# Own weight tiles for chunks of seven products, and a third such chunk in each gate unit

## The chip, the cores and the metric

The kernel runs on one core of one Trainium2 chip. The core has TensorE (PE: matmuls and transposes, which write to PSUM), VectorE (DVE), ScalarE (ACT), GpSimd (POOL) and SyncE (SP, which here issues the loads of weights). Each engine takes the instructions of its own queue in the order in which the program wrote them; this kernel writes that order by hand (`manual_schedule`). The metric is the device time of one execution in microseconds. All times are from the profiled execution or from the table of runs.

## The reference, cut to what matters

One layer of an encoder on 256 tokens with 2048 channels, in float32:

```python
x = x + 0.5 * swiglu(rmsnorm(x, n1), w_gate1, w_up1, w_down1)   # FFN 1, 5632 hidden
...                                                             # mixers: pooling and convolution branches
x = x + 0.5 * swiglu(rmsnorm(x, n2), w_gate2, w_up2, w_down2)   # FFN 2, 5632 hidden
return rmsnorm(x, n_final)

def swiglu(h, w_gate, w_up, w_down):
    return (silu(h @ w_gate) * (h @ w_up)) @ w_down
```

The change touches the two FFNs alone.

## The kernel before

**High and low halves.** Every float32 operand of a matmul is split in two: a high half (a cast to the matmul's type, by ScalarE, L153) and a low half (source minus high, by VectorE, L155). A product is three matmuls: high by high, high by low, low by high. The function is `hi_lo`.

**Chunks.** All weights stream through as chunks of two rows of 128 x 1024 (`raw`, five tiles of 512 KB, loaded by SP two chunks ahead). `run` goes over the stream: at step i it issues the load of chunk i+2, splits chunk i+1 (`split_chunk`), runs the functions that `at(i, ...)` has put aside for this step, and then issues the matmuls of chunk i (`run_chunk`). What `amid(i, ...)` has put aside comes in the middle of these, after the 12th matmul of chunk i. The high and low tiles of a chunk's rows (`wh`, `wl`) have four buffers each, which is two chunks: the split of chunk i+1 waits until TensorE has left chunk i-1.

**Eights and sevens.** An ordinary chunk multiplies two 128-row slices of the activations by a 128 x 1024 weight row each, for two halves of the tokens: eight products of 128 x 128 by 128 x 512, 24 matmuls (L256). A chunk listed in `SEVEN` is taken as a product of 2 x 2 blocks by a scheme with seven products, 21 matmuls (L277). Its price is paid by the other engines: `split_seven` forms three sums of weight blocks with four additions on VectorE (L193, tiles `sum`, in place in `raw` too), then splits row 0, the three sums (`exth`, `extl`, 128 x 1536) and row 1, in this order. The activations need four differences as well, the *E forms* (`e_forms`, L307, then split into `xE` or `hE`), once per FFN. Four of the seven products are shared by several results: they are collected in PSUM banks 0 to 3 (`P1`, `P5`, `P6`, `P7`) over all sevens of a unit, and after the last one `shared_parts` combines them (L427 and L432) into two `part` tiles. The other three products go straight to the accumulators in banks 4 to 7. In a seven the shared products come first (12 matmuls, in the order `P1`, `P5`, `P6`, `P7`; the second matmul of `P6` is the first to need `extl`), except in the first unit after an ordinary one (`u.start`), where they come last.

**Units.** An FFN is a stream of units: eleven gate units (u = 0 to 10, eight chunks each, 512 columns of gate and of up), and down units in between. Gate unit 0 has eights alone; units 1 to 10 have sevens at chunks 0 and 2. After units 4 and 8 come two down units each (eight chunks, sevens at 0 and 2), and after unit 10 the last two (six eights each).

**The end of a gate unit** (`gate_done_seven`): VectorE adds the accumulators of each token half to `part` (L413, 128 x 1024), ScalarE applies silu (L414), VectorE multiplies to the hidden values `h` (L418). The next gate unit transposes them back on TensorE (`put`, L343): two groups of four transposes, into banks `P6` and `P1` as soon as `shared_parts` has read them. Each is split into `ht` by ScalarE and VectorE. For two hidden slices of each four units (u % 4 = 0 and 1, first group) a copy `hy` is made from the same bank (L389) and E forms of it follow at once. `gate_early` puts these two groups at the heads of the two chunks after the one at which it runs; it runs at the step after the unit's last seven, so now they stand at the heads of chunks 4 and 5.

Of the kernel before, what the change touches and what calls it, by code (L numbers as in the profile page):

```python
# [8 lines left out]
F32 = mybir.dt.float32  # L9
F32R = mybir.dt.float32r  # L10
# [3 lines left out]
P = 128  # L14
D = 2048
T = 256
# [10 lines left out]
W2 = 2 * C  # L27
KD = D // P
# [11 lines left out]

GROUP = 4
SEVEN = (0, 2)

B_P1, B_P5, B_P6, B_P7, B_11, B_12, B_21, B_22 = range(8)

# [36 lines left out]
def encoder_kernel(ctx: ExitStack, tc: tile.TileContext, x, xT, vecs, rows, pool_m,  # L82
# [7 lines left out]
    stg = ctx.enter_context(tc.tile_pool(name="stg", bufs=2))  # L90
# [13 lines left out]
    ps = psp.tile([P, 8, C], F32, name="ps")  # L104
# [5 lines left out]
    stream = []  # L110
    side, middle = {}, {}

    def at(i, fn):

        side.setdefault(i, []).append(fn)

    def amid(i, fn):

        while isinstance(stream[i][0], Special):
            i += 1  # L120
        middle.setdefault(i, []).append(fn)
# [6 lines left out]
    def add_unit(u):  # L128
        for cc in range(u.k // 2):
            stream.append((u, cc))  # L130
# [21 lines left out]
    def hi_lo(src, h, l=None):  # L152
        nc.scalar.copy(out=h, in_=src)  # L153
        if l is not None:
            nc.vector.tensor_tensor(out=l, in0=src, in1=h.bitcast(F32), op=ALU.subtract)  # L155
        return h, l

    def stream_tiles(i, kk):
        return (wsp.tile([P, W2], F32R, tag="wh", name=f"wh{i}_{kk}"),
                wsp.tile([P, W2], F32R, tag="wl", name=f"wl{i}_{kk}"))  # L160
# [26 lines left out]
    def split_seven(i, r0, r1):  # L187

        w11, w12, w21, w22 = r0[:, :C], r0[:, C:], r1[:, :C], r1[:, C:]
        sm = ffn["pool"].tile([P, 3, C], F32, tag="sum", name=f"sum{i}")  # L190

        def add(out, a, b):
            nc.vector.tensor_tensor(out=out, in0=a, in1=b, op=ALU.add)  # L193
        add(sm[:, 1, :], w12, w22)
        add(w12, w11, w12)
        add(sm[:, 0, :], w12, w22)
        add(sm[:, 2, :], sm[:, 0, :], w21)
        ext = tuple(ffn["pool"].tile([P, 3, C], F32R, tag=f"ext{x}", name=f"ext{x}{i}") for x in "hl")
        return (hi_lo(r0, *stream_tiles(i, 0)), hi_lo(sm, *ext), hi_lo(r1, *stream_tiles(i, 1)))

    def bank(name):
        Pos.bank += 1
# [79 lines left out]
    def pair(pool, tag, n, name):  # L282

        r = []
        for b in range(n // 4):
            h, l = (block(pool, f"{tag}{s}{b}", F32R, f"{name}{s}{b}") for s in "hl")
            r += [(h[:, q, :], l[:, q, :]) for q in range(4)]
        return r

    def block(pool, tag, dtype, name):  # L290
        return pool.tile([P, 4, T], dtype, tag=tag, name=name)

    def hidden(pool, name):

        return [tuple(block(pool, f"h{s}{u}", F32R, f"{name}{s}{u}") for s in "hl") for u in range(GROUP)]

    def e_tiles(pool, tag, n):

        return {c: tuple(pool.tile([P, 4, P], F32R, tag=f"{tag}E{x}{c}", name=f"{tag}E{x}{c}_{n}") for x in "hl")
                for c in SEVEN}  # L300

    def e_forms(dst, even, odd):

        e = stg.tile([P, 4, P], F32, tag="sg", name=f"e{Pos.now}")
        a11, a21, a12, a22 = even[:, :P], even[:, P:], odd[:, :P], odd[:, P:]
        for n, (a, b) in enumerate(((a11, a21), (a21, a22), (a11, e[:, 1, :]), (a12, e[:, 2, :]))):
            nc.vector.tensor_tensor(out=e[:, n, :], in0=a, in1=b, op=ALU.subtract)  # L307
        hi_lo(e, *dst)
# [16 lines left out]
    def lhs_of(pairs):  # L325
        def f(k, t):
            h, l = pairs[k]
            return h[:, t * P:(t + 1) * P], l[:, t * P:(t + 1) * P]
        return f
# [8 lines left out]
    def transposes(src_of, n, name, b=None):  # L338

        b = bank(name) if b is None else b  # L340
        for j in range(n):
            for t in range(NT):
                nc.tensor.transpose(out=b[:, j * T + t * P: j * T + (t + 1) * P],  # L343
                                    in_=src_of(j, t), identity=ident)
        return b
# [22 lines left out]
    ffn = {}  # L368

    def open_ffn(stack, n):  # L370

        pool = ffn["pool"] = stack.enter_context(tc.tile_pool(name=f"ffn{n}", bufs=1))
        ffn["ht"] = hidden(pool, f"ht{n}")
        ffn["hE"] = e_tiles(pool, "h", n)
        ffn["t0"], ffn["t1"] = (pool.tile([P, 2, C], F32, tag=f"part{t}", name=f"part{n}_{t}") for t in range(NT))

    def ffn_units(w_g, w_d, xt, xE, rs, residual_done, tail=None):
        waiting = []

        def hidden_lhs(k, t):  # L380
            return tuple(h[:, k % 4, t * P:(t + 1) * P] for h in ffn["ht"][k // 4])

        def put(u, hs, k0, b=None):
            b = transposes(lambda j, t: hs[t][:, (k0 + j) * P:(k0 + j + 1) * P], 2, f"hT{Pos.now}_{k0}", b)
            hi_lo(b.rearrange("p (q t) -> p q t", q=2), *(h[:, k0:k0 + 2, :] for h in ffn["ht"][u % GROUP]))
            c = (u % GROUP) * 2 + k0 // 2
            if c in SEVEN:
                y = stg.tile([P, 2, T], F32, tag="sg", name=f"hy{Pos.now}_{k0}")
                nc.scalar.copy(out=y, in_=b.rearrange("p (q t) -> p q t", q=2))  # L389
                e_forms(ffn["hE"][c], y[:, 0, :], y[:, 1, :])  # L390

        def hidden_tile(t):
            return stg.tile([P, C], F32, tag="h", name=f"h{Pos.now}_{t}")

        def gate_done(u):
            def done(acc):
                hs = []
                for t in range(NT):
                    sg = stg.tile([P, C], F32, tag="sg", name=f"sg{Pos.now}_{t}")
                    h = hidden_tile(t)  # L400
                    nc.scalar.activation(sg, acc[t][:, 0, :], AF.Silu, scale=rs[:, t:t + 1])  # L401
                    nc.vector.scalar_tensor_tensor(out=h, in0=acc[t][:, 1, :], scalar=rs[:, t:t + 1],
                                                   in1=sg, op0=ALU.mult, op1=ALU.mult)
                    hs.append(h)
                waiting.append((u, hs))
            return done
# [27 lines left out]
        def gate_early():  # L434
            shared_parts()
            if waiting:
                u, hs = waiting.pop()
                at(Pos.now + 1, lambda: put(u, hs, 0, ps[:, B_P6, :]))
                at(Pos.now + 2, lambda: put(u, hs, 2, ps[:, B_P1, :]))

        def into_residual(t, half, part):
            xs = X[t][:, half * W2:(half + 1) * W2]
# [3 lines left out]
        def down_early(half):  # L446
            def early():
                shared_parts()
                for t in range(NT):
                    at(Pos.now + 1 + t, lambda t=t: into_residual(t, half, ffn[f"t{t}"]))  # L450
            return early
# [16 lines left out]
        def add_down(g, k, last):  # L468
            for half in range(2):
# [3 lines left out]
                else:  # L473
                    add_unit(Unit(w_d[half], k, hidden_lhs, down_done(half, False), k0=g * GROUP * 4,
                                  forms=forms_of(hidden_lhs, LateE()), early=down_early(half), seven=SEVEN))

# [5 lines left out]
        for u in range(units):  # L482
            if u:
                add_unit(Unit(w_g[u], KD, lhs_of(xt), gate_done_seven(u), forms=forms_of(lhs_of(xt), xE),
                              early=gate_early, seven=SEVEN, start=(lambda: None) if u == 1 else None))
            else:
                add_unit(Unit(w_g[u], KD, lhs_of(xt), gate_done(u)))
            if u and u % GROUP == 0:
                add_down(u // GROUP - 1, 4 * GROUP, False)
        add_down((units - 1) // GROUP, 4 * (units - (units - 1) // GROUP * GROUP), True)  # L490
# [13 lines left out]
    xE1 = e_tiles(xtp, "x", 1)  # L504
# [23 lines left out]
    def run(first, last):  # L528
        for i in range(first, last):
            Pos.now = i  # L530
            load(i + PF - 1)
            split_chunk(i + LEAD)
            for fn in side.pop(i, []):
                fn()
            if mix.get("conv_on"):
                conv_some()
            run_chunk(i)


    ht_stack = ExitStack()  # L540
    open_ffn(ht_stack, 1)
    xt2 = pair(xtp, "x", KD, "xt2")
    ffn_units(w_g1, w_d1, xt1, xE1, rstd[0], next_operand(xt2, V_NM, rstd[1]))
    n1 = len(stream)

# [260 lines left out]
    xE3 = {}  # L806
# [71 lines left out]
    at(n3 - 1, final_first_half)  # L878


    xr = [block(ffn["pool"], f"xr{j}", F32, f"xr{j}") for j in range(4)]
    start()
    for i in range(PF - 1):
        load(i)
# [8 lines left out]
    for t in range(NT):  # L893
        at(2 + t, lambda t=t: load_x(t))
    at(KD // 2, lambda: nc.gpsimd.dma_start(out=vec[:, KD:], in_=vecs[:, KD:]))
    for c in SEVEN:
        at(c + 1, lambda c=c: scaled_forms(xE1[c], [xr[c // 2][:, 2 * c % 4 + j, :] for j in range(2)], V_N1, 2 * c))
    run(0, n1)
    ht_stack.close()
# [15 lines left out]

    ht_stack = ExitStack()
    open_ffn(ht_stack, 2)
    run(n2, n3)
    for i in sorted(side):
        for fn in side[i]:  # L920
# [88 lines left out]
```

## Time and profile before

| what | us |
|---|---|
| median of 3 runs | 1945.78 |
| lowest to highest | 1945.39 to 1946.57 |
| profiled execution | 1945.58 |
| its span in the profile | 1943.8 |

The 1.8 us between the last two lie around the span. The granted clock of TensorE was 0.999 of full speed. By the profile FFN 1 lasts from the start to about 721 us and FFN 2 from about 1221 us to the end; the mixers lie between. In the profile a busy row has start, length and the instruction, with the idle time before it and what ended that in brackets. L numbers are lines of the kernel before.

### The profile page before, as it was taken

The numbers are of one execution on the slowest core, as the hardware profiler recorded it, in microseconds if no ns is written. First come the engines' busy times: TensorE is split into PE (matmuls) and PEld (weight loads), VectorE is DVE, ScalarE is ACT, GpSimd is POOL, SyncE is SP. The second block draws the span as 40 slices with busy tenths as digits, with TensorE's granted clock in tenths as the row PEclk, the third lists the DMA queues.
The fourth block names the chain that finished last, engine by engine and source line by source line (L and its number), as shares of the span: only waits on it lengthen the run. The fifth ranks groups of instructions, "written<-read, shape, count | busy, mean of one in ns | idle before, by whom it ended". The sixth has DMA issues, their size and how long they took to land.

```text
span 1943.8 us, 23272 instructions
## 1 busy us (share of the span) xinstructions
PE 1931.8 (99%) x8680; PEld 1597.5 (82%) x8680; DVE 1520.0 (78%) x1762; ACT 975.7 (50%) x1117; POOL 11.3 (1%) x22
## 2 busy tenths in 40 slices
PE   9999999999999999999999999999999999999998
PEld 7888888888888888888888888888888888888886
DVE  6888888888888555888888766688888888888855
ACT  6555544554545454454444545455554455554544
POOL 0000000000000000000000000000000000000000
PEclk9999999999999999999999999999999999999999
DMA  8555566655665556566666555555656665566664
GB/s 316 191 183 198 193 216 192 203 190 190 198 204 201 189 188 202 189 200 208 204 206 200 190 184 185 183 194 179 201 196 215 191 199 193 186 201 203 197 194 147
DMA packets 106145, 383.90 MB, mean 198 GB/s; under 512 B 11920, under 2 KB 12176, under 8 KB 105776
## 3 DMA queue, kind: packets, MB, share of 16 engines
q1 hardware_dynamic: 104688, 378.45, 59.2%
q0 software_dynamic: 1056, 3.83, 0.6%
q8 instruction: 68, 1.11, 0.2%
q14 instruction: 45, 0.37, 0.1%
q10 hardware_dynamic: 288, 0.14, 0.0%
HBM read 380.28 MB, written 2.10 MB: 197 GB/s over the span
## 4 chain that ended last, share of the span: by engine, by line
PE 98%; DVE 1%; issue 0%; ACT 0%; DMA 0%; DVEq 0%; POOLq 0%; POOL 0%; ACTq 0%
PE ps L256 82%; PE ps L277 13%; PE ps L343 2%; PE ps L741 0%; DVE wl L155 0%; DMA xr<-in_xT 0%; DVE sum L193 0%; PE ps L716 0%; ACT exth L153 0%; ACT wh L153 0%; DVE extl L155 0%; DVE raw L193 0%; ACT fsq L850 0%; ACT sg L401 0%; PE ps L623 0%
## 5 line engine op out<-in xcount | busy, mean ns | idle before, releaser
L153 ACT CAST wh<-raw 128x1024 fp32r<-128x1024 f32 (+1 forms) x706 | 726.5, 1048 | 710.9 <-PE ps L256 393.9
L155 DVE TENSOR_TENSOR wl<-raw,wh 128x1024 fp32r<-128x1024 f32 (+1 forms) x706 | 844.5, 1218 | 300.4 <-ACT wh L153 297.4
L256 PE MATMUL ps<-wh,xt1h 128*128 128x512 f32 x544 | 170.6, 395 | 1.2 <-ACT wh L153 1.2
L256 PE MATMUL ps<-wh,xt3h 128*128 128x512 f32 x544 | 169.6, 393 | 0.0
L256 PE MATMUL ps<-wl,xt1h 128*128 128x512 f32 x544 | 168.4, 391 | 0.0
L256 PE MATMUL ps<-wh,xt1l 128*128 128x512 f32 x544 | 168.0, 390 | 0.0
L256 PE MATMUL ps<-wl,xt3h 128*128 128x512 f32 x544 | 167.9, 390 | 0.0
L256 PE MATMUL ps<-wh,xt3l 128*128 128x512 f32 x544 | 167.6, 389 | 0.0
L256 PE MATMUL ps<-wh,xt2h 128*128 128x512 f32 x448 | 138.4, 390 | 0.0
L256 PE MATMUL ps<-wl,xt2h 128*128 128x512 f32 x448 | 138.1, 389 | 0.0
L256 PE MATMUL ps<-wh,xt2l 128*128 128x512 f32 x448 | 137.9, 389 | 0.0
L256 PEld LDWEIGHTS ps<-wl,xt1h 128*128 128x128 f32 x544 | 102.6, 189 | 21.9 <-DVE wl L155 0.3
L256 PEld LDWEIGHTS ps<-wh,xt1l 128*128 128x128 f32 x544 | 102.4, 188 | 21.6
L256 PEld LDWEIGHTS ps<-wh,xt3l 128*128 128x128 f32 x544 | 102.1, 188 | 21.7
L256 PEld LDWEIGHTS ps<-wl,xt3h 128*128 128x128 f32 x544 | 102.1, 188 | 21.5
L256 PEld LDWEIGHTS ps<-wh,xt1h 128*128 128x128 f32 x544 | 101.1, 189 | 21.4 <-ACT wh L153 1.7
L155 DVE TENSOR_TENSOR extl<-sum,exth 128x1536 fp32r<-128x1536 f32 x56 | 98.5, 1759 | 25.4 <-ACT exth L153 25.4
L256 PEld LDWEIGHTS ps<-wh,xt3h 128*128 128x128 f32 x544 | 100.5, 188 | 19.5
L256 PEld LDWEIGHTS ps<-wl,xt2h 128*128 128x128 f32 x448 | 84.1, 188 | 17.7
L256 PEld LDWEIGHTS ps<-wh,xt2l 128*128 128x128 f32 x448 | 84.1, 188 | 17.5
L600 DVE SCALAR_TENSOR_TENSOR conv<-gluT,vec,conv 128x241 f32<-128x241 f32 (+14 forms) x240 | 96.9, 471 | 0.0
L256 PEld LDWEIGHTS ps<-wh,xt2h 128*128 128x128 f32 x448 | 83.3, 188 | 16.5
(237 smaller groups left out, 2851.9 us busy)
## 6 DMA issues: line engine op xcount, KB each, us to landing
raw<-in_w_g SPq DMA_DIRECT2D x350, 512.0 KB, 4.2
raw<-in_w_d SPq DMA_DIRECT2D x176, 512.0 KB, 4.0
raw<-in_w_in SPq DMA_DIRECT2D x112, 512.0 KB, 3.9
raw<-in_w_out SPq DMA_DIRECT2D x32, 512.0 KB, 3.5
raw<-in_w_pp SPq DMA_DIRECT2D x16, 512.0 KB, 3.7
raw<-in_w_cp SPq DMA_DIRECT2D x16, 512.0 KB, 3.8
row<-in_rows POOLq DMA_DIRECT2D x7, 512.0 KB, 4.0
X<-in_x SPq DMA_DIRECT2D x2, 1024.0 KB, 8.7
```

Of the source, the lines that this page charges most:

```text
L153: nc.scalar.copy(out=h, in_=src)
L155: nc.vector.tensor_tensor(out=l, in0=src, in1=h.bitcast(F32), op=ALU.subtract)
L256: nc.tensor.matmul(u.acc[t + c if u.tail and t else t][:, c, :], lhsT=a, rhs=b[:, c * C:(c + 1) * C], start=(t, c) not in u.begun, stop=k ...
L277: nc.tensor.matmul(ps[:, b, :], lhsT=x_, rhs=w_, start=where not in u.begun, stop=b < B_11 and cc == u.seven[-1] and n == 2)
L343: nc.tensor.transpose(out=b[:, j * T + t * P: j * T + (t + 1) * P], in_=src_of(j, t), identity=ident)
L600: nc.vector.scalar_tensor_tensor(out=dst, in0=src, scalar=w, in1=dst, op0=ALU.mult, op1=ALU.add)
```

## The change

It has five parts:

1. Gate units 1 to 10 take `SEVEN_GATE = (0, 2, 4)`: a third chunk of seven products, at chunk 4. Down units keep `SEVEN = (0, 2)`. A third set of E forms of the normed input is needed (`xE`, chunk 4), made in gate unit 0 of FFN 1 and ahead of gate unit 1 of FFN 2.
2. The rows of a seven are split into tiles of their own (`rowh0`, `rowl0`, `rowh1`, `rowl1`, one buffer each) instead of `wh` and `wl`. The four buffers of these now serve the eights alone.
3. The two transpose groups of `gate_early` go through `amid` into the middle of one chunk, both together. As the unit's last seven is now chunk 4, this is chunk 6.
4. `hy` has a tile of its own in place of one of `sg`, and its E forms come four steps after the copy, which is step 2 of the next unit.
5. The tiles of the hidden values are taken at the end of gate unit 0, and the raw input of FFN 1 (`xr`) stands in their place until then.

```diff
+SEVEN_GATE = (0, 2, 4)
...
-        return (hi_lo(r0, *stream_tiles(i, 0)), hi_lo(sm, *ext), hi_lo(r1, *stream_tiles(i, 1)))
+        rows = [tuple(ffn["pool"].tile([P, W2], F32R, tag=f"row{x}{kk}", name=f"row{x}{i}_{kk}") for x in "hl")
+                for kk in range(2)]
+        return (hi_lo(r0, *rows[0]), hi_lo(sm, *ext), hi_lo(r1, *rows[1]))
...
-        ffn["ht"] = hidden(pool, f"ht{n}")
+        ffn["xE"] = e_tiles(pool, "x", n, SEVEN_GATE[2:])
...
+        def open_hidden():
+            ffn["ht"] = hidden(ffn["pool"], f"ht{stream.index((first, 0))}")
...
-                y = stg.tile([P, 2, T], F32, tag="sg", name=f"hy{Pos.now}_{k0}")
+                y = ffn["pool"].tile([P, 2, T], F32, tag="y", name=f"hy{Pos.now}_{k0}")
                 nc.scalar.copy(out=y, in_=b.rearrange("p (q t) -> p q t", q=2))
-                e_forms(ffn["hE"][c], y[:, 0, :], y[:, 1, :])
+                at(Pos.now + 4, lambda: e_forms(ffn["hE"][c], y[:, 0, :], y[:, 1, :]))
...
-                at(Pos.now + 1, lambda: put(u, hs, 0, ps[:, B_P6, :]))
-                at(Pos.now + 2, lambda: put(u, hs, 2, ps[:, B_P1, :]))
+                amid(Pos.now + 1, lambda: put(u, hs, 0, ps[:, B_P6, :]))
+                amid(Pos.now + 1, lambda: put(u, hs, 2, ps[:, B_P1, :]))
...
-                              early=gate_early, seven=SEVEN, start=(lambda: None) if u == 1 else None))
+                              early=gate_early, seven=SEVEN_GATE, start=(lambda: None) if u == 1 else None))
...
-                add_unit(Unit(w_g[u], KD, lhs_of(xt), gate_done(u)))
+                first = Unit(w_g[u], KD, lhs_of(xt), gate_done(u))
+                add_unit(first)
+                at(len(stream), open_hidden)
...
-    xr = [block(ffn["pool"], f"xr{j}", F32, f"xr{j}") for j in range(4)]
+    xr = [block(ffn["pool"], f"h{x}{j}", F32, f"xr{x}{j}") for j in (2, 3) for x in "hl"]
...
-    for c in SEVEN:
+    for c in SEVEN_GATE:
         at(c + 1, lambda c=c: scaled_forms(xE1[c], [xr[c // 2][:, 2 * c % 4 + j, :] for j in range(2)], V_N1, 2 * c))
```

`e_tiles` takes the list of chunks as an argument, and `xE1` and `xE3` get the third set from the FFN's pool.

More of the change, by code (lines that the diff above doesn't have):

```diff
@@ L295, in hidden, with e_tiles @@
         return [tuple(block(pool, f"h{s}{u}", F32R, f"{name}{s}{u}") for s in "hl") for u in range(GROUP)]
-    def e_tiles(pool, tag, n):
+    def e_tiles(pool, tag, n, pairs=SEVEN):
         return {c: tuple(pool.tile([P, 4, P], F32R, tag=f"{tag}E{x}{c}", name=f"{tag}E{x}{c}_{n}") for x in "hl")
-                for c in SEVEN}
+                for c in pairs}
     def e_forms(dst, even, odd):
@@ L541, in encoder_kernel @@
     open_ffn(ht_stack, 1)
+    xE1.update(ffn["xE"])
     xt2 = pair(xtp, "x", KD, "xt2")
@@ L917, in encoder_kernel @@
     open_ffn(ht_stack, 2)
+    xE3.update(ffn["xE"])
     run(n2, n3)
```

## The prediction

> **What bounds the kernel now.** I read the page's busy shares and its chain of work that ended last, then the waits of TensorE's weight loader (PEld), then one gate unit in the chain and in the timelines.
>
> ```profile
> PE 1931.8 (99%) x8680; PEld 1597.5 (82%) x8680; DVE 1520.0 (78%) x1762; ACT 975.7 (50%) x1117; POOL 11.3 (1%) x22
> PE 98%; DVE 1%; issue 0%; ACT 0%; DMA 0%; DVEq 0%; POOLq 0%; POOL 0%; ACTq 0%
> PEld ps L277 <- DVE extl L155: 4.5, 19, 0.7
> ```
>
> TensorE is the bound: 98% of the chain, and its largest steady wait is 4.5 us in all. That wait is for `extl`, the low half of the three summed weight tiles of a chunk of seven, which VectorE writes. So VectorE already arrives a hair late there. Next, one gate unit, 43.20 us of chunks 0 to 7, with sevens at chunks 0 and 2 (columns of the chain: start, length, work; of the windows: stretch, length, then busy time by engine):
>
> ```profile
> 139.62 4.76 PE ps L277 x21
> 144.38 5.44 PE ps L256 x24
> 149.82 4.85 PE ps L277 x21
> ...
> 166.48 16.34 PE ps L256 x72
> 139.62:182.82 43.20, 43.20 (x195) 35.60 (x195) 35.20 (x36) 22.02 (x24) 0.00 (x0) 1.00 0.58 194
> 353.57:396.78 43.21, 43.21 (x195) 35.61 (x195) 36.90 (x41) 22.97 (x26) 0.00 (x0) 1.00 0.59 195
> ```
>
> A matmul takes 5.44/24 = 0.227 us. An eight costs 5.44, a seven 4.76; the 4.85 of chunk 2 holds 0.09 of that wait. The two groups of transposes take 43.20 - 2 x 4.76 - 6 x 5.44 - 0.09 = 0.95 us. VectorE is busy 35.20 us of 43.20, and 36.90 in a unit that also makes E forms of the hidden values (second window row).
>
> **The change, part by part.** (1) *The gain.* 20 gate units (ten per FFN) turn one eight into a seven: 20 x (5.44 - 4.76) = 13.6 us less on TensorE. The unit becomes 3 x 4.76 + 5 x 5.44 + 0.95 = 42.43 us.
>
> (2) *VectorE's work.* Its rows around the unit's start, in program order (start, length, instruction):
>
> ```profile
> 131.05 0.68 DVE L193 TENSOR_TENSOR sum<-raw,raw 128x512 f32<-128x512 f32 x1
> ...
> 135.46 1.76 DVE L155 TENSOR_TENSOR extl<-sum,exth 128x1536 fp32r<-128x1536 f32 x1 [0.41 <-ACT exth L153]
> 137.14 1.22 DVE L155 TENSOR_TENSOR wl<-raw,wh 128x1024 fp32r<-128x1024 f32 x1
> 138.28 1.22 DVE L413 TENSOR_TENSOR part<-ps,part 128x1024 f32<-128x1024 f32 x1
> 139.66 1.23 DVE L413 TENSOR_TENSOR part<-ps,part 128x1024 f32<-128x1024 f32 x1 [0.16 <-PE ps L256]
> 140.80 1.63 DVE L418 SCALAR_TENSOR_TENSOR h<-part,rstd 128x512 f32<-128x512 f32 x2
> 142.62 2.36 DVE L155 TENSOR_TENSOR wl<-raw,wh 128x1024 fp32r<-128x1024 f32 x2 [0.19 <-ACT wh L153]
> 144.89 0.68 DVE L193 TENSOR_TENSOR sum<-raw,raw 128x512 f32<-128x512 f32 x1
> ...
> 149.39 1.76 DVE L155 TENSOR_TENSOR extl<-sum,exth 128x1536 fp32r<-128x1536 f32 x1 [0.50 <-ACT exth L153]
> 151.24 0.46 PE L277 MATMUL ps<-extl,xEh 128*128 128x512 f32 x1
> ```
>
> From start to start: splitting a seven takes 138.28 - 131.05 = 7.23 us, an eight 144.89 - 142.62 = 2.27. So a third seven adds about 5 us per unit to an engine with 8 idle: it still fits by busy time (35.20 + 5 < 42.43). Whether it fits in time depends on what pins it.
>
> (3) *The transposes of the hidden values* move from the heads of chunks 4 and 5 to after the 12th matmul of chunk 6, both together. VectorE's two `ht` subtractions move with them, and in VectorE's queue they stand before the split of the next unit's chunk 0. Now that split starts early: 131.05 is 8.6 us before the unit ends at 139.62. After the change it waits for the transposes. Rows of a transpose group, and of one that also copies `hy` and makes E forms:
>
> ```profile
> 159.95 0.60 PE L343 MATMUL ps<-ident,h 128*128 128x128 f32 x4
> 74.68 0.58 ACT L153 CAST ht1h<-ps 128x512 fp32r<-128x512 f32 x1
> 76.67 0.59 ACT L389 COPY hy<-ps 128x512 f32<-128x512 f32 x1 [1.41 <-DVE ht1l L155]
> 75.95 0.68 DVE L155 TENSOR_TENSOR ht1l<-ps,ht1h 128x512 fp32r<-128x512 f32 x1
> 77.29 0.49 DVE L307 TENSOR_TENSOR e<-hy 128x128 f32<-128x128 f32 x2 [0.66 <-ACT hy L389]
> ...
> 79.12 0.69 DVE L155 TENSOR_TENSOR hEl<-e,hEh 128x512 fp32r<-128x512 f32 x1 [0.69 <-ACT hEh L153]
> ```
>
> Transposes 0.60, cast 0.58, two subtractions 0.60 apart (queued instructions overlap by 0.08) and two hand-overs of 0.04: VectorE comes to the next split 2.45 us after the first transpose starts. That holds **VectorE's chain in a plain unit**: 2.45, split of chunk 0 7.23, first add into `part` 1.14 (139.66 to 140.80), second add to the split of chunk 2 5.23 (139.66 to 144.89), that split to the end of `extl` 6.26 (144.89 to 151.15). Sum 22.3 us. **TensorE over the same stretch**: transposes 0.95, rest of chunk 6 2.72, chunk 7 5.44, chunks 0 and 1 4.76 + 5.44, seven matmuls of chunk 2 1.59, then it needs `extl`. Sum 20.9. TensorE waits **1.4 us**. The wait moves its transposes, so VectorE is pinned anew each unit and never gets ahead. Eight units per two FFNs are such: those after gate units 3, 4, 7, 8 of each.
>
> (4) *`hy` and the E forms.* In units 1, 2, 5, 6, 9 the `hy` copy stands between the two `ht` casts, and it waits until `ht1l` has been read (the 76.67 row: 76.63 is the end of that subtraction). So cast, subtraction, copy, second cast and its subtraction follow one another: 3.70 us in place of 2.45. Four steps on, after the split of chunk 3 in the following unit, stand the E forms: 77.29 to 79.12 + 0.60 = 2.43 us, ahead of the new seven at chunk 4. Chain to the `extl` of chunk 4: 3.70 + 7.23 + 1.14 + 5.23 + 7.23 + 2.27 + 2.43 + 6.26 = 35.5. TensorE: 20.9 with the other 3.17 of chunk 2, 5.44 of chunk 3, 1.59 into chunk 4 = 31.1. It waits **4.4 us** in each of ten units (2, 3, 6, 7, 10 of both FFNs). A plain unit's chunk 4 adds nothing: 22.3, the last 0.97 of that split, an eight's 2.27 and 6.26 are 31.8, under 31.1 + 1.4. Units 5 and 9 stand behind down units, which transpose nothing, and behind unit 10 come only eights: no wait there.
>
> The Trainium skill, "PSUM — Partial Sum Buffer", section "PSUM bank collisions raise a hardware error", says that two engines must not touch one bank at once, "reads against reads included", so software keeps them apart; the 76.67 row agrees. Were the two reads allowed together, ten units would save some 0.7 us each.
>
> (5) *Own tiles for the sevens.* ScalarE's casts now wait for TensorE to leave a chunk:
>
> ```profile
> ACT wh L153 <- PE ps L256: 393.9, 255, 3.1
> ```
>
> Much of that goes, and weights can be split a chunk earlier. But ScalarE is half idle, and the row is worth only what TensorE itself waits: 0.09 in 19 places (the loader runs ahead of the matmuls, so its own 4.5 us are more), 1.7 us. I take the 1.7 as a gain, because (3) and (4) count their waits in full; the ends are 0 and 1.7.
>
> (6) *Start of FFN 1.* A third set of x forms is made in unit 0, steps 5 and 6, right ahead of unit 1's first split.
>
> ```profile
> 27.08 0.89 ACT L322 ACTIVATE y<-xr,vec 128x256 f32<-128x256 f32 x2
> 45.42 0.17 DVE L363 TENSOR_SCALAR msq<-msq 128x2 f32<-128x2 f32 x1
> 45.50 0.69 DVE L193 TENSOR_TENSOR sum<-raw,raw 128x512 f32<-128x512 f32 x1
> 52.89 0.47 PE L277 MATMUL ps<-wl,xt1h 128*128 128x512 f32 x1
> ```
>
> That split starts at 45.50 straight behind VectorE's last statistic, and TensorE waits for its `wl` at 52.89 already (0.47 for 0.39): no slack. 0.89 + 2.43 = 3.3 us, once. In FFN 2 the forms are made three chunks before unit 1, where eights leave VectorE idle: 0.
>
> (7) `hidden` allocated later, `xr` in its tiles: no instruction, 0.
>
> *Sum*: -13.6 - 1.7 + 8 x 1.4 (11.2) + 10 x 4.4 (44) + 3.3 = +43.2 us. The profiled execution took 1945.58 us (its span 1943.8 and 1.8 around it), 0.2 under the median of 1945.78. 1945.6 + 43.2 = **1989 us**, 2.2% slower.
>
> **The rivals.** *A: VectorE's slack swallows it, faster.* By busy time it fits (40 of 42.43), so if the `ht` subtractions do not hold the next split, everything hides: 1945.6 - 13.6 - 1.7 + 3.3 (6) at most = 1931 to 1934. For it: 8 us idle per unit. Against: the idle time lies where VectorE waits for weight casts, ahead of the split at 131.05, and the moved subtractions put the pin behind it. It decides if the plain chain is under 20.9 instead of 22.3, and the other under 31.1 instead of 35.5. 12%.
>
> *B: only the plain pin costs.* The E forms and `hy` fall into waits that I have not seen (VectorE running ahead in chunks 2 to 4): 18 x 1.4 = 25, so 1945.6 - 15.3 + 25.2 + 3.3 = 1959. For it: a chain of 35 us leaves more room for error than one of 22. Against: no instruction of it waits for TensorE. 15%.
>
> *C: loads come late too.* Five raw tiles hold two and a half chunks, and a raw tile comes free only when VectorE has split it.
>
> ```profile
> raw<-in_w_g SPq DMA_DIRECT2D x350, 512.0 KB, 4.2
> ```
>
> A load lands after 4.2 us; by (4) the tightest, the second raw tile of chunk 4, has some 8 us between the split that frees its buffer and its own. If loads queue and that fails, about 1 us more in each of 18 units: 2007. 8%.
>
> That the change does not do what it says I leave aside: chunks and their order are written out.
>
> The Trainium skill, "TensorE: Matmul & The Clock Gate", Part 1, states that TensorE falls to half speed after about 3.4 us without work. My longest single wait, 3.3 us in (6), comes near; an estimate by that page is 1.7 us more, once.
>
> **How the numbers follow.** Forecast 62%, its own range 1975 to 2000 (0.5 us either way in each of 18 waits, and 6 us for E forms); A 12%, B 15%, C 8%; 3% for about no change. The range reaches down past B and up towards C: 1953 to 2003. A measurement of this kernel can tell about 0.2%, 3.9 us, from no change. Faster 12%, within 3%, slower 85%.
>
> **What would show it.** Right: 8620 matmuls (60 fewer); three L277 groups per gate unit; plain units of 43.8 us, those with E forms of 46.8; PEld's wait for `extl` grown from 4.5 to tens of us; VectorE's split of chunk 0 starting after the transposes of chunk 6 and its `part` adds ending 2 to 4 us after TensorE has begun the next unit. Wrong: units of 42.4 us with no wait for `extl` or `wl` (A); units with E forms no longer than the others (B); ScalarE or VectorE waiting for DMA of `raw` (C).

## The result, and the profile after

| | median us | lowest to highest | ratio to before, 95% interval |
|---|---|---|---|
| before | 1945.71 | 1945.39 to 1946.57 | |
| after | 1993.46 | 1992.60 to 1994.92 | 1.0245 (1.0228 to 1.0263) |

The changed kernel is 2.4% slower; 1989 us was forecast. Its profiled execution took 1992.6 us, of which 1990.8 are the span; that is 47.0 us over the span of before. First the page after: busy shares, then the chain of work that ended last.

```profile
PE 1938.7 (97%) x8620; PEld 1582.8 (80%) x8620; DVE 1604.1 (81%) x1872; ACT 999.5 (50%) x1143; POOL 11.1 (1%) x22
PE 71%; DVE 17%; ACT 7%; issue 4%; DMA 1%; ACTq 0%; DVEq 0%; POOLq 0%; POOL 0%
```

TensorE does 60 matmuls less, as it should. But its part of the chain has fallen from 98% to 71%, and VectorE (17%) and ScalarE (7%) stand in it now. The busy time of TensorE has even risen by 7 us. The records of matmuls overlap, 0.39 us each with 0.227 from start to start, and a matmul ahead of a wait counts with its whole 0.39. The waits of its weight loader, then of TensorE itself (total, times, longest):

```profile
PEld ps L280 <- DVE extl L156: 27.7, 30, 1.6
PEld ps L280 <- DVE part L419: 22.7, 18, 1.8
PEld ps L280 <- DVE rowl L156: 12.1, 13, 1.1
PEld ps L259 <- DVE wl L156: 10.8, 19, 0.6
```

```profile
PE ps L280 <- DVE part L419: 15.1, 18, 1.4
PE ps L280 <- DVE extl L156: 15.0, 30, 1.3
PE ps L280 <- DVE rowl L156: 6.5, 12, 0.6
PE ps L259 <- DVE wl L156: 2.5, 15, 0.2
```

Before, the first view had 4.5 us for `extl` and little else, the second 0.3. All four writers are VectorE's (L280, L259, L419 and L156 are L277, L256, L413 and L155 of before). `part` comes 18 times: the adds that must free the accumulators end too late at 18 unit starts, eight plain ones and ten with E forms. Two gate units in the windows, unit 2 of FFN 1 (with `hy` before it and E forms in it) and unit 4 (plain):

```profile
98.67:145.76 47.09, 43.97 (x193) 34.80 (x191) 40.97 (x47) 24.35 (x26) 0.00 (x0) 1.00 0.54 179
192.80:236.85 44.05, 43.30 (x192) 34.95 (x191) 39.20 (x42) 23.14 (x24) 0.00 (x0) 1.00 0.57 191
```

They last 47.09 and 44.05 us, where 46.8 and 43.8 were forecast. VectorE is idle for 5 to 6 us in each and sets the time all the same. The granted clock stays at 1.00. Where unit 2 loses its time, in TensorE's timeline (in brackets the idle time ahead and what ended it):

```profile
102.94 0.50 PE L280 MATMUL ps<-exth,xt1h 128*128 128x512 f32 x1 [1.39 <-DVE part L419]
105.90 0.72 PE L259 MATMUL ps<-wl,xt1h 128*128 128x512 f32 x2 [0.16 <-DVE wl L156]
113.20 0.50 PE L280 MATMUL ps<-extl,xEh 128*128 128x512 f32 x1 [0.42 <-DVE extl L156]
122.96 0.50 PE L280 MATMUL ps<-rowl,xt1h 128*128 128x512 f32 x1 [0.58 <-DVE rowl L156]
125.20 0.50 PE L280 MATMUL ps<-extl,xEh 128*128 128x512 f32 x1 [0.57 <-DVE extl L156]
```

There is one wait at each place that the chain of (3) and (4) passes: the accumulators in chunk 0, the weights of chunk 1, `extl` of chunk 2, and row 0 and `extl` of chunk 4, behind the E forms. And VectorE at the end of that unit, from the transposes (TensorE starts them at 136.71) to the next unit:

```profile
137.96 0.69 DVE L156 TENSOR_TENSOR ht0l<-ps,ht0h 128x512 fp32r<-128x512 f32 x1 [1.47 <-ACT ht0h L154]
139.80 0.69 DVE L156 TENSOR_TENSOR ht0l<-ps,ht0h 128x512 fp32r<-128x512 f32 x1 [1.14 <-ACT ht0h L154]
140.40 0.68 DVE L194 TENSOR_TENSOR sum<-raw,raw 128x512 f32<-128x512 f32 x1
...
147.62 2.35 DVE L419 TENSOR_TENSOR part<-ps,part 128x1024 f32<-128x1024 f32 x2
```

It stands idle 1.47 and 1.14 us with the next unit's split right behind it in its queue; the split starts at 140.40, 3.69 us after the transposes, and the `part` adds at 147.62, 1.86 us after TensorE has begun the next unit (145.76). The forecast had 3.70 for the first. The adds end at 149.97, 4.2 us into the next unit, and 3.0 us into it behind the plain unit 4; the forecast had 2 to 4 us.

### The profile page after: what moved, and what is told of

Same layout as the page of the kernel before. It is cut to its first block, busy times and chain, and to the rows that moved or that the text cites. A ratio compares the mean times of both kernels' runs of the same rounds, so it can differ in the third digit from the quotient of the medians.

```text
span 1990.8 us, 23189 instructions
## 1 busy us (share of the span) xinstructions
PE 1938.7 (97%) x8620; PEld 1582.8 (80%) x8620; DVE 1604.1 (81%) x1872; ACT 999.5 (50%) x1143; POOL 11.1 (1%) x22
## 4 chain that ended last, share of the span: by engine, by line
PE 71%; DVE 17%; ACT 7%; issue 4%; DMA 1%; ACTq 0%; DVEq 0%; POOLq 0%; POOL 0%
PE ps L259 59%; PE ps L280 10%; DVE sum L194 5%; DVE extl L156 3%; ACT exth L154 3%; DVE wl L156 2%; DVE part L419 2%; ACT wh L154 2%; DVE raw L194 2%; PE ps L346 1%; DVE rowl L156 1%; ACT rowh L154 1%; DVE e L310 1%; DVE ht0l L156 0%; DVE ht222l L156 0%
## 5 line engine op out<-in xcount | busy, mean ns | idle before, releaser
L156 DVE TENSOR_TENSOR wl<-raw,wh 128x1024 fp32r<-128x1024 f32 (+1 forms) x554 | 657.6, 1217 | 217.5 <-ACT wh L154 216.5
L154 ACT CAST wh<-raw 128x1024 fp32r<-128x1024 f32 (+1 forms) x554 | 562.3, 1046 | 427.9 <-PE ps L259 350.4
L154 ACT CAST rowh<-raw 128x1024 fp32r<-128x1024 f32 x152 | 159.5, 1050 | 234.9 <-DVE raw L194 226.1
L156 DVE TENSOR_TENSOR rowl<-raw,rowh 128x1024 fp32r<-128x1024 f32 x152 | 185.2, 1218 | 0.1
L156 DVE TENSOR_TENSOR extl<-sum,exth 128x1536 fp32r<-128x1536 f32 x76 | 133.7, 1759 | 34.9 <-ACT exth L154 34.9
L259 PE MATMUL ps<-wh,xt1h 128*128 128x512 f32 x464 | 144.9, 394 | 1.0 <-ACT wh L154 1.0
L259 PE MATMUL ps<-wl,xt1h 128*128 128x512 f32 x464 | 144.2, 392 | 1.2 <-DVE wl L156 1.2
L259 PE MATMUL ps<-wl,xt3h 128*128 128x512 f32 x464 | 143.8, 391 | 1.0 <-DVE wl L156 0.7
L259 PE MATMUL ps<-wh,xt3h 128*128 128x512 f32 x464 | 144.0, 392 | 0.0
L259 PE MATMUL ps<-wh,xt1l 128*128 128x512 f32 x464 | 143.5, 391 | 0.0
L259 PE MATMUL ps<-wh,xt3l 128*128 128x512 f32 x464 | 143.0, 389 | 0.0
L259 PE MATMUL ps<-wh,xt2h 128*128 128x512 f32 x448 | 138.4, 390 | 0.0
L259 PE MATMUL ps<-wl,xt2h 128*128 128x512 f32 x448 | 138.1, 389 | 0.0
L259 PE MATMUL ps<-wh,xt2l 128*128 128x512 f32 x448 | 137.9, 389 | 0.0
L154 ACT CAST exth<-sum 128x1536 fp32r<-128x1536 f32 x76 | 112.7, 1482 | 27.4 <-DVE sum L194 25.9
L194 DVE TENSOR_TENSOR sum<-raw,raw 128x512 f32<-128x512 f32 x152 | 104.6, 688 | 2.6
L259 PEld LDWEIGHTS ps<-wl,xt1h 128*128 128x128 f32 x464 | 86.9, 188 | 22.1 <-DVE wl L156 4.4
L259 PEld LDWEIGHTS ps<-wl,xt3h 128*128 128x128 f32 x464 | 86.5, 188 | 21.7 <-DVE wl L156 4.0
L259 PEld LDWEIGHTS ps<-wh,xt1l 128*128 128x128 f32 x464 | 87.3, 188 | 18.7 <-DVE xt1l L338 0.5
L259 PEld LDWEIGHTS ps<-wh,xt1h 128*128 128x128 f32 x464 | 86.8, 189 | 19.0 <-ACT wh L154 1.5
L259 PEld LDWEIGHTS ps<-wh,xt3l 128*128 128x128 f32 x464 | 87.1, 188 | 18.3
L259 PEld LDWEIGHTS ps<-wh,xt3h 128*128 128x128 f32 x464 | 86.2, 188 | 17.3
```

Source lines behind the costliest of these rows:

```text
L259: nc.tensor.matmul(u.acc[t + c if u.tail and t else t][:, c, :], lhsT=a, rhs=b[:, c * C:(c + 1) * C], start=(t, c) not in u.begun, stop=k ...
```

## The experiments

Each is an edit of the changed kernel: of one to three lines in `puts_head`, `hy_last`, both `two_sevens`, `shared_tiles` and `head_hylast`, of some more in the others. The row numbers of their traces are those of the changed kernel, some lines on. A unit's time is from the first matmul of its chunk 0 to that of the next unit; without waits it is 3 x 4.76 + 5 x 5.44 + 0.88 (the eight transposes together) = 42.36 us.

**puts_head: transposes 2.7 us earlier**

```diff
-                amid(Pos.now + 1, lambda: put(u, hs, 0, ps[:, B_P6, :]))
-                amid(Pos.now + 1, lambda: put(u, hs, 2, ps[:, B_P1, :]))
+                at(Pos.now + 1, lambda: put(u, hs, 0, ps[:, B_P6, :]))
+                at(Pos.now + 1, lambda: put(u, hs, 2, ps[:, B_P1, :]))
```

> Both transpose groups come at the head of chunk 6 instead of its middle, 2.72 us earlier; nothing else differs from the changed kernel (1993.5 us). Theory (VectorE's queue is pinned by the moved transposes): the wait of the eight plain units (1.65 us each) goes to 0, that of the ten units with E forms falls from 4.7 to about 2.0 (the E forms' 1.8 ahead of chunk 4 stay): 1993.5 - 13 - 27 = 1954 us, between 1950 and 1960. Rival (VectorE has too much work per unit, wherever it stands): the same instructions, so within 3 us of 1993.5.

Measured 1964.59 us (1964.37 to 1965.06). The same instructions in the same number run 29 us faster, so the place of the pin decides and not the amount of work: that rival falls. The plain units are free of waits, as expected. But units with E forms last 45.48 us, 1.1 more than expected, and this is why 1954 was missed. ScalarE's and VectorE's timelines right ahead of such a unit, at the end of unit 1, where the transposes start at 87.20:

```profile
87.40 1.05 ACT L154 CAST wh<-raw 128x1024 fp32r<-128x1024 f32 x1 [1.67 <-PE ps L259]
```

```profile
88.48 1.23 DVE L156 TENSOR_TENSOR wl<-raw,wh 128x1024 fp32r<-128x1024 f32 x1 [1.49 <-ACT wh L154]
89.62 0.68 DVE L156 TENSOR_TENSOR ht0l<-ps,ht0h 128x512 fp32r<-128x512 f32 x1
```

The second row of chunk 7 is cast only when TensorE leaves chunk 5, since eights still have buffers for two chunks. That split stands ahead of the `ht` subtractions and is a second pin, which puts the first subtraction 1.2 us later than the transposes alone would (0.60 + 0.58 and two hand-overs after 87.20, against 89.62). The expectation had overlooked it.

**hy_last: the group with the copy second**

```diff
-                amid(Pos.now + 1, lambda: put(u, hs, 0, ps[:, B_P6, :]))
-                amid(Pos.now + 1, lambda: put(u, hs, 2, ps[:, B_P1, :]))
+                amid(Pos.now + 1, lambda: put(u, hs, 2, ps[:, B_P1, :]))
+                amid(Pos.now + 1, lambda: put(u, hs, 0, ps[:, B_P6, :]))
```

> The two transpose groups change places in the middle of chunk 6: the one with the hy copy comes second, so that no ht cast stands behind the copy. Theory: the chain from the transposes to VectorE's next split falls from 3.70 to 2.45 us in ten units: 1.25 x 10 = 12.5 us less, 1981 us, and the units with E forms wait about 3.4 instead of 4.7 us. Rival (the copy does not really wait for VectorE's read of the bank): 0.5 x 10 = 5 us less, 1988. Rival of too much work: 1993, the same instructions.

Measured 1980.27 us (1980.07 to 1980.99), 13.2 less; unit 2 lasts 45.80 us, so it waits 3.4 us. The 1.25 us of `hy` are as (4) had them, and the copy does wait for VectorE's read of the same bank.

**two_sevens and two_sevens_b: the change without its third seven**

```diff
-SEVEN_GATE = (0, 2, 4)
+SEVEN_GATE = (0, 2)
...
-                at(Pos.now + 4, lambda: e_forms(ffn["hE"][c], y[:, 0, :], y[:, 1, :]))
+                at(Pos.now + 2, lambda: e_forms(ffn["hE"][c], y[:, 0, :], y[:, 1, :]))
```

`two_sevens_b` has `Pos.now + 1` in the last line.

> All of the change but the third chunk of seven: gate units take sevens at chunks 0 and 2 again, with tiles of their own; the transposes then stand in the middle of chunk 4, and the E forms two steps after the copy (step 6), where VectorE has room. Theory: no wait is left, 1945.7 - 1.8 (old waits for extl) - 1.4 (transposes together) = 1942.5 us. Rival (tiles with one buffer hold up the splits): slower than 1947.

> As two_sevens, but the E forms stand one step after the copy (step 5), so that they are no longer between the split of chunk 7, which waits for chunk 5's buffers, and the split of the next unit's chunk 0. Theory: two_sevens lost its 2.2 us in each of ten units to that place alone; they go: 1966.4 - 22 = 1944 us or a little under. Rival (the own tiles or the joint transposes cost something by themselves): 1950 or more.

Measured 1966.39 us (1966.15 to 1966.69) for the first, a miss by 24 us, and 1944.35 us (1943.92 to 1944.98; ratio to before 0.9993, 0.9984 to 1.0003) for the second. In the trace of the first, the units right behind E forms last 45.31 us and the others 43.12. VectorE ahead of the longer ones:

```profile
86.75 1.23 DVE L156 TENSOR_TENSOR wl<-raw,wh 128x1024 fp32r<-128x1024 f32 x1 [1.50 <-ACT wh L154]
87.89 0.49 DVE L310 TENSOR_TENSOR e<-hy 128x128 f32<-128x128 f32 x2
...
89.72 0.69 DVE L156 TENSOR_TENSOR hEl<-e,hEh 128x512 fp32r<-128x512 f32 x1 [0.69 <-ACT hEh L154]
90.32 0.68 DVE L194 TENSOR_TENSOR sum<-raw,raw 128x512 f32<-128x512 f32 x1
```

It is the pin of `puts_head` again, the second row of chunk 7, and the E forms between it and the next unit's split: 2.2 us in each of ten units. One step earlier they stand ahead of that pin and cost nothing. So the other parts of the change, with the E forms in that place, are worth about 1 us together, if anything. The third seven isn't needed for a loss, as the first of the two runs shows: what costs time is work that comes late in VectorE's queue, and in the changed kernel it is the third seven that pushes it there.

**shared_tiles: the third seven without tiles of its own**

```diff
-        rows = [tuple(ffn["pool"].tile([P, W2], F32R, tag=f"row{x}{kk}", name=f"row{x}{i}_{kk}") for x in "hl")
-                for kk in range(2)]
+        rows = [stream_tiles(i, kk) for kk in range(2)]
```

> All of the change but the own tiles: sevens take wh and wl again. Theory: VectorE is late at every place where TensorE waits, so the buffers are free by then and it makes no difference: 1993.5 within 3 us. Rival (the own tiles are what makes a third seven possible): the splits wait for buffers on top of the rest, 2003 us or more.

Measured 1992.34 us (1991.85 to 1992.60; ratio 1.0239, 1.0223 to 1.0254), the time of the changed kernel within its interval. The own tiles, the first part of the change's name, make no difference in this kernel. No run takes them out of the faster orders below, so whether they matter there stays open.

**eforms_pool: the E forms on GpSimd**

```diff
-    def e_forms(dst, even, odd):
+    def e_forms(dst, even, odd, eng=None):
+
+        eng = eng or nc.vector
...
-            nc.vector.tensor_tensor(out=e[:, n, :], in0=a, in1=b, op=ALU.subtract)
-        hi_lo(e, *dst)
+            eng.tensor_tensor(out=e[:, n, :], in0=a, in1=b, op=ALU.subtract)
+        nc.scalar.copy(out=dst[0], in_=e)
+        eng.tensor_tensor(out=dst[1], in0=e, in1=dst[0].bitcast(F32), op=ALU.subtract)
...
-                at(Pos.now + 4, lambda: e_forms(ffn["hE"][c], y[:, 0, :], y[:, 1, :]))
+                at(Pos.now + 4, lambda: e_forms(ffn["hE"][c], y[:, 0, :], y[:, 1, :], nc.gpsimd))
```

> The changed kernel (1993.5 us) with the E forms of the hidden values computed on GpSimd (four differences and the low half), which takes 2.43 us out of VectorE's queue ahead of chunk 4 in ten units; nothing else moves. Theory: the 1.8 us wait at chunk 4 goes in ten units, the 2.9 us at chunks 0 to 2 stay: 1975 us, and units after the copy last 45.4 instead of 47.1. Rival (GpSimd's reads slow VectorE down, or the chain is not in order): above 1985.

Measured 1983.41 us (1982.93 to 1983.62): 10 us less, not 18; units of 46.08 us. GpSimd's one long instruction and VectorE beside it:

```profile
115.69 1.77 POOL L314 TENSOR_TENSOR hEl<-e,hEh 128x512 fp32r<-128x512 f32 x1 [20.61 <-ACT hEh L313]
```

```profile
115.10 3.44 DVE L156 TENSOR_TENSOR wl<-raw,wh 128x1024 fp32r<-128x1024 f32 x2
...
125.75 2.36 DVE L156 TENSOR_TENSOR wl<-raw,wh 128x1024 fp32r<-128x1024 f32 x2
```

The same two subtractions take 3.44 us beside GpSimd and 2.36 without it. So 1.08 us come back: chunk 4 now takes 5.22 us instead of 6.56 and still waits some 0.46. The differences of the E forms, which GpSimd makes as soon as it has the copy, likewise lengthen two additions of the next split (0.92 and 0.83 us for 0.69), and chunk 0 takes 6.85 us instead of 6.45. The second of VectorE's two subtractions ends 1.08 us after GpSimd's (118.54 against 117.46), which is about what one takes alone (1.14 from start to start). The Trainium skill, "SBUF — State Buffer", section "SBUF: two separate sides", calls the ports that VectorE and GpSimd share an exclusive lock; these rows agree.

**head_hylast and all_pool: the pins put right**

`head_hylast` joins the edits of `puts_head` and `hy_last`; `all_pool` adds the E forms on GpSimd, those of the input too.

> Both transpose groups at the head of chunk 6, the one with hy second; E forms still on VectorE ahead of chunk 4. Theory: no wait at chunks 0 to 2 but for the old 0.1, since the split of chunk 0 starts over 8 us before the unit ends; at chunk 4 the E forms leave 1.8 to 2.0 us in ten units: 1945.5 - 13.6 - 1.4 + 3.4 (start of FFN 1) + 19 = 1953 us. Rival (VectorE's sum of work is the bound, 43.8 us in these units): 1956 or more and waits that stay at chunks 0 to 2.

> head_hylast with all E forms on GpSimd, those of the input too. Theory: the waits are gone, the gain of the third seven is left: 1945.5 - 13.6 - 1.4 + 1 (start of FFN 1) = 1931.5 us, gate units of 42.4 us. Rival (VectorE has no room left, or GpSimd disturbs it): gate units of 43 us or more, 1943 or slower.

`head_hylast` measured 1952.32 us (1951.50 to 1952.88), as expected: unit 2 lasts 44.27 us, and the wait that is left is at chunk 4. `all_pool` measured 1943.51 us (1942.91 to 1944.05) where 1931.5 was expected, as its rival (GpSimd disturbs VectorE) has it; its units with E forms last 43.26 us, because VectorE is lengthened in them as in `eforms_pool` (in unit 2 the subtraction beside GpSimd's long one takes 2.31 us instead of 1.22, and three rows of the split ahead of it 0.1 to 0.3 us more each), and the start of FFN 1 has not become shorter.

**spread, spread_start, spread_all: the E forms in two parts behind chunk 4**

The transposes are as in `head_hylast`. Differences five steps after the copy, cast and low half one later:

```diff
-    def e_forms(dst, even, odd):
+    def e_forms(dst, even, odd, later=None):
...
-        hi_lo(e, *dst)
+        if later:
+            later(Pos.now + 1, lambda: hi_lo(e, *dst))
+        else:
+            hi_lo(e, *dst)
...
-                at(Pos.now + 4, lambda: e_forms(ffn["hE"][c], y[:, 0, :], y[:, 1, :]))
+                at(Pos.now + 5, lambda: e_forms(ffn["hE"][c], y[:, 0, :], y[:, 1, :], at))
```

In `spread_start` the forms of the input and the statistic of FFN 1 move, in `spread_all` the order of the split of chunk 0 as well:

```diff
-            at(4 + t, lambda half=half: squares(t, 2 * half, half * W2, (half + 1) * W2))
+            at(4 + 2 * t, lambda half=half: squares(t, 2 * half, half * W2, (half + 1) * W2))
...
-            at(6, lambda: finish_rstd(rstd[0]))
+            at(7, lambda: finish_rstd(rstd[0]))
...
-        at(c + 1, lambda c=c: scaled_forms(xE1[c], [xr[c // 2][:, 2 * c % 4 + j, :] for j in range(2)], V_N1, 2 * c))
+        at(min(c + 1, 4), lambda c=c: scaled_forms(xE1[c], [xr[c // 2][:, 2 * c % 4 + j, :] for j in range(2)], V_N1, 2 * c))
...
+        if stream[i][1] == 0:
+            a, c = hi_lo(r0, *rows[0]), hi_lo(r1, *rows[1])
+            return (a, hi_lo(sm, *ext), c)
```

> head_hylast with the E forms of the hidden values in two parts behind the split of chunk 4: the differences at step 3 of the next unit, the cast and the low half at step 4, so that VectorE does not idle 0.6 us for the cast and no E form stands ahead of a seven. VectorE's sum in these units falls from 43.8 to 43.2 us against TensorE's 42.4. Theory: in the ten units some 0.3 to 0.8 us of waits are left (at chunks 0 to 2 of the unit behind), in place of 1.8: 1945.5 - 13.6 - 1.4 + 3.3 (start) + 3 to 8 = 1937 to 1942 us. Rival (the place does not matter, the sum does, with nothing hidden): 1950 as in head_hylast.

> As spread, with the third set of x forms one step earlier in unit 0 of FFN 1 (step 4 and 5), and the squares of the second token half and the statistic behind them one or two steps later, so that VectorE makes these forms where it waited for ScalarE's squares. Theory (the start of FFN 1 costs about 3 us because the forms stand right ahead of unit 1's first split): 2 to 3 us less than spread, all of it ahead of 75 us. Rival (the start is bound by loads): no difference.

> As spread_start, with the split of a unit's chunk 0 in the order row 0, row 1, sums, so that VectorE does not wait 0.4 us for the cast of the sums there; extl then ends about as late as the split did before, ahead of its use in all but the first unit. Theory: the waits left at chunks 0 to 2 fall by up to 0.4 us in ten units, 0 to 4 us less than spread_start; in FFN 1's and FFN 2's unit 1, which need the sums first, up to 1 us more each.

`spread` measured 1936.68 us (1936.20 to 1937.33), a little under its 1937 to 1942, `spread_start` 1936.58 (1936.37 to 1936.82), `spread_all` 1933.57 (1933.06 to 1934.97; ratio to before 0.9940, 0.9923 to 0.9956). Unit 3 in `spread`, then units 3 and 2 in `spread_all`; all three have E forms:

```profile
141.51:184.36 42.85, 42.71 (x192) 35.10 (x191) 40.68 (x47) 23.68 (x25) 0.00 (x0) 1.00 0.62 196
```

```profile
140.96:183.42 42.46, 42.46 (x192) 35.10 (x191) 40.59 (x47) 23.57 (x25) 0.00 (x0) 1.00 0.61 201
98.49:140.96 42.47, 42.47 (x192) 35.10 (x191) 40.52 (x46) 24.06 (x26) 0.00 (x0) 1.00 0.60 196
```

VectorE is busy for 40.6 us here and for 40.97 in the changed kernel's unit of 47.09. So nearly the same work fits into 42.46 us, once it stands in the right order; 0.1 us of waits is left per unit. In `spread` unit 2 is as short (42.43); the 0.4 us more of unit 3 are in its chunk 2, as it stands behind another unit with E forms.

`spread_start` gains nothing, where 2 to 3 us were expected: it begins the transposes of unit 1 at 87.38 us, `spread` at 87.31. Its first half was right: unit 1's first seven starts at 52.58 instead of 53.23 and takes 6.92 instead of 8.24 us. But its second seven, chunk 2, now takes 6.80 instead of 4.76 (all from TensorE's timelines), since the statistic comes late and ScalarE waits for it:

```profile
55.80 1.26 ACT L410 ACTIVATE sg<-ps,rstd 128x512 f32<-128x512 f32 x2 [1.85 <-POOL rstd L371]
```

The wait moved. So the rival (loads) isn't what keeps the time there, and what the start costs at the least remains open. Of the 3.0 us between `spread_start` and `spread_all`, 2.4 are eight units (3, 4, 7 and 8 of each FFN, each behind one with E forms), whose chunk 2 waits some 0.3 us less. The other 0.7 are at the start of FFN 1, where the expectation had up to 1 us more: unit 2 begins at 98.49 instead of 99.15.

## Why the prediction was right

Step by step; the measured sums are from the two traces of before and after.

| step | forecast | measured |
|---|---|---|
| (1) twenty sevens for eights | -13.6 | -13.6 (4.76 and 5.44 stand unchanged) |
| (3) wait of a plain unit, 8 times | 1.4 | 44.05 - 42.36 = 1.7 |
| (4) wait of a unit with E forms, 10 times | 4.4 | 47.09 - 42.36 = 4.7 |
| (5) old waits for `extl` gone | -1.7 | some -1.8: none of the old waits is left beside the new ones |
| (6) start of FFN 1 | +3.3 | +3.2 |
| transposes together | 0 | 0.95 to 0.88, 20 times: -1.4 |

The measured terms add up to -13.6 + 13.6 + 47 - 1.8 + 3.2 - 1.4 = 47.0 us, the difference of the spans.

**The bound** was read rightly: the 4.5 us for `extl` marked the place that had no slack, and the first three waits grew there and ahead of it. **The pin** of step (3) is shown by `puts_head`, where it alone moves and 29 us go, and by `spread`, where the work stays and the waits go. **`hy`** is shown by `hy_last`. **The E forms** ahead of chunk 4 are shown by `head_hylast`: chunk 4 takes 6.55 us there instead of 4.76, and these 1.8 are what the sum has for them (4.4 less 1.4 and the 1.25 of `hy`). `spread`, which moves only these forms, gains 15.6 us on it. **The own tiles** were costed at almost nothing, and `shared_tiles` shows nothing.

**The sizes** were 0.3 us short in both kinds of unit, 5 us in all. VectorE's chain was exact: 3.69 us for 3.70, and 7.22 to the `part` adds for 7.23. What the sum left out is on TensorE's side: the restart. The end of `extl` in chunk 4 of unit 2, on VectorE, and the matmul behind the one that waited for it:

```profile
123.38 1.76 DVE L156 TENSOR_TENSOR extl<-sum,exth 128x1536 fp32r<-128x1536 f32 x1 [0.48 <-ACT exth L154]
```

```profile
125.54 0.40 PE L280 MATMUL ps<-exth,xEl 128*128 128x512 f32 x1
```

`extl` ends at 125.14, its matmul starts at 125.20, and the next stands 0.34 us behind that instead of 0.227. The sum had let the wait end with the writer. That is 0.2 of the 0.3. Another 0.07 is the transposes' 0.88 for 0.95: they shorten TensorE's own stretch, and where VectorE sets the unit's length, the wait grows by as much (the table has it in its last row). The rest I did not trace.

**What the forecast overlooked**: some of the E forms are for nothing. Sets of the hidden values of units 8 and 9 are made too, but the last down units, which take these values, have eights alone. In FFN 1 the last matmul that reads `hE` starts at 561.9 us, and VectorE still writes such sets at 651.3 (in unit 10) and at 693.8; in FFN 2 it is the same. Without the copy and the forms unit 10 would be a plain unit, which waits 1.7 us instead of 4.7; by this estimate some 6 of the 47 us went, over both FFNs, to forms that no matmul reads. No run leaves them out.

**Rival A** (slack) took VectorE's busy time for the measure; it fails at the pin. (The lower end of its range is 1930 by its own terms, not 1931.) **Rival B** (only the plain pin) fails on 47.09 against 44.05. **Rival C** (late loads) fails too: in the waits of TensorE, its loader and VectorE no DMA stands, ScalarE waits 4.0 us in all for loads of gate weights, before 3.9, and such a load lands in 4.1 us, before in 4.2.

**The clock**: the granted clock shows 1.00 in the windows and 0.999 for the run, as before. The start of FFN 1 did not lose its 3.2 us in one wait: TensorE's longest there is 1.29 us, and in the whole run 1.4. So no run here shows what the Trainium skill, "TensorE: Matmul & The Clock Gate", Part 1, says of longer ones.

## What to carry to other kernels

Before work is added to an engine that looks a fifth idle, add up its own queue, with its hand-overs, from the last instruction at which another engine holds it to the first that the bound engine needs, and set that against the bound engine's time over the same stretch. An instruction that is moved later in one queue holds up all that stands behind it there, so look at what follows it, not only at what it does. If a change is slower, try the same work in another order before giving it up: here the same sevens give 1933.6 us instead of 1993.5, by the transposes at the chunk's head, the copy last, the E forms split up behind the seven and one split reordered.

## What had not been expected of the hardware

- GpSimd is no free place for VectorE's work: a subtraction of 1.77 us on GpSimd lengthened VectorE's two by 1.08 us, and 2.43 us taken off VectorE brought 1.0 us per unit.
- TensorE's restart after a wait costs more than the wait: the matmul at which it ends has its successor 0.34 us behind it, not 0.227.
